# Attention with keys on partitions: scores computed transposed, the row maximum subtracted inside the fifth score pass

## The chip, the core and the metric

The kernel runs on one NeuronCore of a Trainium2 chip, as one program. The metric is the device time of one execution in microseconds. The median of three runs of the kernel before is given below, and beside it the time of the one execution that was profiled. In the profile PE is TensorE's matmul stream and PEld its weight loads, DVE is VectorE, ACT is ScalarE, POOL is GpSimd, SP is SyncE, which issues the DMAs.

## The reference, cut to what matters

The model is a two-layer backbone over 1024 latent tokens and 256 context tokens of width 1024. Layer 0 is a bidirectional gated linear recurrence (HGRN2), layer 1 is multi-head latent attention with 16 heads. Only the attention of layer 1 is touched. For each head it computes, with a score scale of (128 + 64) ** -0.5:

```python
s = (jnp.einsum('bqhd,bkhd->bhqk', q_nope, k_nope, preferred_element_type=jnp.float32)
     + jnp.einsum('bqhr,bkr->bhqk', q_pe, k_pe, preferred_element_type=jnp.float32))
p = jax.nn.softmax(s * MLA_SCALE, axis=-1)
return jnp.einsum('bhqk,bkhd->bqhd', p.astype(v.dtype), v)
```

Queries are the 1024 latent tokens (8 tiles of 128), keys are all 1280 tokens (10 tiles of 128). The output of each head is multiplied by a SiLU gate `z` and goes into the last projection `w_mo`.

## The kernel before

Products that must keep float32 accuracy are made of three passes: each operand is split into a high part in `float32r` and a low part (the rest), and `mm3` (line 261) adds high x high, low x high and high x low in PSUM. `split` (line 208) makes the parts: ScalarE copies the high part, VectorE subtracts it. The keys are shared by all heads, since the key projection is absorbed into the queries: `kh` and `kl` are the parts of the latent keys with their 128 channels on partitions, `kr` holds the rope keys, high part in partitions 0 to 63 and low part in 64 to 127. `vh` and `vl` are the latent values, with tokens on partitions.

The program runs through the stages one after the other: HGRN2, its output projection, `mla_in` (line 670: latent keys, values and query latents), `mla_rope` and `mla_z` (rope queries and gates, both put into DRAM), then `attend` (line 930), and the last projection.

`attend` writes the order of the attention stage by hand. Every step of four generators gets a due time in units of a query tile; the steps are sorted by it and run, and TensorE keeps that order (`AT_ORDER`, line 1284). The order of VectorE, ScalarE, GpSimd and SP is chosen by the framework, with two priorities (`AT_PRIO`, `EXP_PRIO`) as hints. The generators are:

- `attn_prep` (line 783), once a head: loads the head's weights `wk`, its gates `z` and, for every second head, the rope queries `qr`; forms the absorbed weight (line 800), transposes rope queries (line 818) and splits them into `rh` and `rl`, with a copy of the high part in the other partition half on GpSimd (`TWIN`, line 826); and forms the absorbed queries `qah` and `qal`.
- `attn_scores` (line 839), once a query tile: three blocks of keys (512, 512 and 256 columns), each with five matmuls (lines 855 to 859) whose stationary operand is the query tile, so that the scores lie with queries on partitions and keys along the row. VectorE reduces each block (line 861) and joins the three (line 867). The scale is negative, so the minimum is taken and handed to the exponential as a bias (line 871), and ScalarE's accumulator gives the row sums. VectorE then multiplies the 1280 probabilities by the reciprocal of the sum (line 882).
- `attn_values` (line 885), once a unit of two query tiles: five times four transposes of probabilities by TensorE (line 902) into `pt`, their split into `ph` and `pl` from PSUM, and six matmuls into `pv`. Then ScalarE copies the result and its high part (lines 920 and 921), GpSimd forms the low part `ol` (line 922), three matmuls apply the value projection, VectorE multiplies by `z` (line 927), and the result is stored in DRAM.
- `tail`: the first half of the last projection for two token tiles, woven into the end of the stage.

PSUM has eight banks of 512 float32 a partition: four for scores (`s`), three for `pt`, one for `pv`.

Of the kernel before, what the change touches and what calls it, by code (L numbers as in the profile page):

```python
# [18 lines left out]
P = 128  # L19
# [18 lines left out]
class Net:  # L38
# [631 lines left out]
    def mla_in(self, pool, pp, kp, a, hh, hl, st):  # L670
# [6 lines left out]
        for c in range(NT):  # L677
# [39 lines left out]
            )  # L717
            if lat:
# [64 lines left out]
    def attn_prep(self, pool, pp, a, st, qrD, zT, h, box):  # L783
# [23 lines left out]
        if h % 2 == 0:  # L807
# [6 lines left out]
            for b, n in self.qgs:  # L814
                sl = slice(b * P, (b + n) * P)
                ps = t(pp, [P, 512], F32, G_TAG)
                for j in range(n):
                    nc.tensor.transpose(ps[:, j * P : (j + 1) * P], qr[:, b + j], self.ident)
                for i, (rh, rl) in enumerate(box["pair"]):
                    own, twin = (slice(0, 64), slice(64, P))[:: 1 - 2 * i]  # L820
                    src = ps[own, : n * P]
                    nc.scalar.activation(rh[own, sl], src, AF.Copy, scale=SCALE)
# [16 lines left out]
    def attn_scores(self, pool, pp, st, box, i, prs):  # L839
        nc, t, NT = self.nc, self.t, self.NT  # L840
        mm = nc.tensor.matmul
        LK = NT * P
        blocks = [(o, min(512, LK - o)) for o in range(0, LK, 512)]
        nb = len(blocks)
        h, j = divmod(i, self.NL)
        qah, qal, rh, rl = box[h][:4]
        js = slice(j * P, (j + 1) * P)
        mx = t(pool, [P, 4], F32, "mx")
        sm = t(pool, [P, 4], F32, "sm")
        pr = t(pool, [P, LK], F32, "pr")  # L850
        sc = []
        for b, (o, w) in enumerate(blocks):
            s = t(pp, [P, 512], F32, "s")
            ks = slice(o, o + w)
            mm(s[:, :w], qah[:, js], st["kh"][:, ks], start=True, stop=False)  # L855
            mm(s[:, :w], qah[:, js], st["kl"][:, ks], start=False, stop=False)  # L856
            mm(s[:, :w], qal[:, js], st["kh"][:, ks], start=False, stop=False)  # L857
            mm(s[:, :w], rh[:, js], st["kr"][:, ks], start=False, stop=False)  # L858
            mm(s[:, :w], rl[:, js], st["kr"][:, ks], start=False, stop=True)  # L859
            with self.tc.high_priority(offset=AT_PRIO):  # L860
                nc.vector.tensor_reduce(mx[:, b : b + 1], s[:, :w], AX.X, ALU.min)  # L861
            sc.append(s)
            if b < nb - 1:
                yield
        nm = t(pool, [P, 1], F32, "nm")
        with self.tc.high_priority(offset=AT_PRIO):
            nc.vector.tensor_reduce(nm, mx[:, :nb], AX.X, ALU.min)  # L867
        for b, (o, w) in enumerate(blocks):
            yield
            with self.tc.high_priority(offset=EXP_PRIO):  # L870
                nc.scalar.activation(  # L871
                    pr[:, o : o + w], sc[b][:, :w], AF.Exp, bias=nm, scale=-1.0,
                    accum_out=sm[:, b : b + 1],
                )
        yield
        rs = t(pool, [P, 1], F32, "rs")
        nc.vector.tensor_reduce(rs, sm[:, :nb], AX.X, ALU.add)
        nc.vector.reciprocal(rs, rs)
        if i % NORM_ACT[1] < NORM_ACT[0]:
            nc.scalar.activation(pr, pr, AF.Copy, scale=rs)  # L880
        else:
            nc.vector.tensor_scalar(pr, pr, rs, None, ALU.mult)
        prs[i] = pr

    def attn_values(self, pool, pp, st, box, u, prs, yT):
        nc, t, NT = self.nc, self.t, self.NT
        tiles = [i for i in (2 * u, 2 * u + 1) if i < self.NH * self.NL]
        h, b = divmod(tiles[0], self.NL)
        n = len(tiles)
        N = n * P  # L890
        wvh, wvl, z = box[h][4:]
        np_ = -(-NT // 2)
        parts = {}
        acc = None
        for e in range(np_ + PV_LAG):
            if e < np_:
                m = min(2, NT - 2 * e)
                tp = t(pp, [P, 2, 2 * P], F32, "pt")
                for c in range(m):
# [491 lines left out]
```

## Time and profile before

| what | value |
|---|---|
| median of the runs | 3146.2 us (3143.35 to 3147.53, 3 runs) |
| time of the profiled execution | 3146.84 us |
| its span, first to last instruction | 3145.1 us |
| mean granted TensorE clock | 0.995 |
| busy share PE, DVE, ACT, POOL | 99%, 69%, 55%, 6% |
| first and last score matmul of the attention stage | 2130.8 and 2949.2 us |
| DMA, mean | 70 GB/s |

A row of a timeline gives start, duration, engine, line, operation, the tiles that it writes and reads, their shape, and in brackets the idle time ahead of it with its releaser. A row for one line gives the count, then the shortest, median and longest duration in nanoseconds, and the first and last start. Matmuls overlap in TensorE's pipeline, so the distance between two starts is the cost of one in a dense stream. A duration on VectorE or GpSimd runs from dispatch to completion and can hold waiting time. `f32` in a shape also stands for `float32r` operands of a matmul.

### The profile page before, as it was taken

The page shows a single profiled execution, that of the slowest core. Times are in us where ns is not written, and L with a number is a line of the kernel's source. Part 1 is how long each engine was busy: PE and PEld are TensorE (multiplying, and loading weights), DVE is VectorE, ACT ScalarE, POOL GpSimd, SP SyncE. Part 2 cuts the span into 40 slices and gives each one's busy share as a digit, 9 for nine tenths or more (in the row PEclk, how much of TensorE's full clock was granted, in tenths as well). Part 3 has the DMA queues.
Part 4 walks back from the last instruction along what each step waited for, and adds up shares of the span by engine and source line. Part 5 has one row for each costly group of instructions (what it writes and reads, how often), then busy time and mean ns, then how long its engine had stood idle before and what let it go on. Part 6 is the DMA issues. An engine that isn't in the chain of part 4 may idle for free.

```text
span 3145.1 us, 51475 instructions
## 1 busy us (share of the span) xinstructions
PE 3108.3 (99%) x19412; PEld 2782.5 (88%) x19412; DVE 2164.4 (69%) x4898; ACT 1729.6 (55%) x4263; POOL 188.3 (6%) x305
## 2 busy tenths in 40 slices
PE   8899999999999999999999999999999999999999
PEld 7889989899898998988988888788999999999887
DVE  7777688776886758757585563536777777777642
ACT  6556465564655646655475563224666666666532
POOL 0000000000000000000000011000010000000000
PEclk8999999999999999999999999999999999999999
DMA  5110212102111021010127661430101011101261
GB/s 212 43 56 23 74 36 63 56 23 75 36 56 57 24 73 36 30 40 25 41 69 243 222 197 45 141 117 24 41 30 38 24 34 34 34 28 38 69 219 57
DMA packets 100009, 218.88 MB, mean 70 GB/s; under 512 B 10289, under 2 KB 47409, under 8 KB 99761
## 3 DMA queue, kind: packets, MB, share of 16 engines
q1 hardware_dynamic: 99760, 215.59, 21.1%
q8 instruction: 153, 2.51, 0.3%
q14 instruction: 96, 0.78, 0.1%
HBM read 175.70 MB, written 39.85 MB: 69 GB/s over the span
## 4 chain that ended last, share of the span: by engine, by line
PE 92%; DVE 3%; issue 2%; DMA 2%; ACT 1%; POOL 0%; SPq 0%; DVEq 0%; POOLq 0%; ACTq 0%
PE g L265 12%; PE g L264 12%; PE g L263 12%; PE lv L335 6%; PE pt L902 4%; PE o L486 3%; PE pv L263 2%; PE s L855 2%; PE pv L264 2%; PE pv L265 2%; PE s L856 2%; PE s L858 2%; PE s L859 2%; PE s L857 2%; PE lv L263 2%; PE lv L265 2%
## 5 line engine op out<-in xcount | busy, mean ns | idle before, releaser
L263 PE MATMUL g<-hh,wh 128*128 128x512 f32 (+1 forms) x1512 | 548.4, 363 | 3.3 <-DVE hh L253 1.6
L265 PE MATMUL g<-hl,wh 128*128 128x512 f32 (+1 forms) x1512 | 542.4, 360 | 3.0 <-DVE hl L254 3.0
L264 PE MATMUL g<-hh,wl 128*128 128x512 f32 (+1 forms) x1512 | 543.3, 359 | 0.0
L263 PEld LDWEIGHTS g<-hh,wh 128*128 128x128 f32 x1512 | 286.5, 189 | 40.6 <-DVE hh L253 2.0
L265 PEld LDWEIGHTS g<-hl,wh 128*128 128x128 f32 x1512 | 285.7, 189 | 39.0 <-DVE hl L254 3.8
L215 DVE TENSOR_TENSOR wl<-raw,wh 128x1024 fp32r<-128x1024 f32 (+1 forms) x170 | 207.7, 1224 | 160.8 <-ACT wh L214 149.4
L264 PEld LDWEIGHTS g<-hh,wl 128*128 128x128 f32 x1512 | 286.4, 189 | 35.9
L861 DVE TENSOR_REDUCE mx<-s 128x1 f32<-128x512 f32 (+1 forms) x384 | 229.7, 599 | 94.5 <-PE s L859 93.0
L871 ACT ACTIVATE pr<-s,nm 128x512 f32<-128x512 f32 (+1 forms) x384 | 232.7, 615 | 99.1 <-DVE nm L867 92.8
L335 PE MATMUL lv<-QX,KX 128*128 128x128 f32 x1920 | 263.1, 275 | 5.8 <-ACT QX L407 4.3
L335 PEld LDWEIGHTS lv<-QX,KX 128*128 128x128 f32 x1920 | 246.6, 192 | 14.8 <-ACT QX L407 5.5
L214 ACT CAST wh<-raw 128x1024 fp32r<-128x1024 f32 (+1 forms) x170 | 178.0, 1049 | 121.8 <-PE lv L264 38.2
L214 ACT CAST ph<-pt 128x512 fp32r<-128x512 f32 x320 | 187.8, 587 | 96.2 <-PE pt L902 86.6
L215 DVE TENSOR_TENSOR pl<-pt,ph 128x512 fp32r<-128x512 f32 x320 | 219.4, 686 | 12.6 <-ACT ph L214 12.5
L263 PE MATMUL g<-wh,hh 128*128 128x256 f32 (+2 forms) x676 | 197.6, 293 | 0.0
L263 PE MATMUL pv<-ph,vh 128*128 128x256 f32 x640 | 196.7, 307 | 0.0
L265 PE MATMUL g<-wl,hh 128*128 128x256 f32 (+2 forms) x676 | 196.4, 291 | 0.0
L902 PE MATMUL pt<-ident,pr 128*128 128x128 f32 x1280 | 192.5, 273 | 0.1
L264 PE MATMUL g<-wh,hl 128*128 128x256 f32 (+1 forms) x654 | 187.9, 287 | 0.0
L407 ACT COPY KX<-K 128x256 f32<-128x256 f32 (+1 forms) x288 | 109.6, 381 | 131.3 <-PE lv L335 71.3
L265 PE MATMUL pv<-pl,vh 128*128 128x256 f32 x640 | 180.2, 282 | 0.0
L264 PE MATMUL pv<-ph,vl 128*128 128x256 f32 x640 | 180.0, 281 | 0.0
(557 smaller groups left out, 7918.3 us busy)
## 6 DMA issues: line engine op xcount, KB each, us to landing
raw<-in_w_o SPq DMA_DIRECT2D x64, 512.0 KB, 3.8
raw<-in_w_qfbz SPq DMA_DIRECT2D x61, 512.0 KB, 3.8
raw<-in_ada_wT SPq DMA_DIRECT2D x32, 512.0 KB, 3.6
raw<-in_w_mo SPq DMA_DIRECT2D x24, 512.0 KB, 3.9
raw<-in_w_v SPq DMA_DIRECT2D x16, 512.0 KB, 3.6
yT<-Z SPq DMA_DIRECT2D x32, 256.0 KB, 2.0
raw<-in_w_z SPq DMA_DIRECT2D x16, 512.0 KB, 4.1
pyr<-yT SPq DMA_DIRECT2D x64, 128.0 KB, 3.7
```

The costliest lines, as they stand in the source:

```text
L214: nc.scalar.copy(hi, src)
L215: (eng or nc.vector).tensor_tensor(lo, src, v32(hi), ALU.subtract)
L263: mm(ps, lh, rh, start=first, stop=False)
L264: mm(ps, ll, rh, start=False, stop=False)
L265: mm(ps, lh, rl, start=False, stop=last)
L335: nc.tensor.matmul(ps[:, sl], lhs[:, sl], rhs[:, sl], start=True, stop=True)
L407: cp(m12(N[:]), m12(Y))
L486: nc.tensor.matmul(o[:, sl], l, r, start=i == 0, stop=i == len(ops) - 1)
L855: mm(s[:, :w], qah[:, js], st["kh"][:, ks], start=True, stop=False)
L861: nc.vector.tensor_reduce(mx[:, b : b + 1], s[:, :w], AX.X, ALU.min)
L871: nc.scalar.activation(pr[:, o : o + w], sc[b][:, :w], AF.Exp, bias=nm, scale=-1.0, accum_out=sm[:, b : b + 1],)
L902: nc.tensor.transpose(tp[:, c, j * P : (j + 1) * P], prs[i][:, k * P : (k + 1) * P], self.ident)
```

## The change

The attention is written anew, in units of two query tiles of one head (64 units).

- `attn_scores` takes a block of two key tiles at a time, five blocks a unit. The stationary operand is now the key tile (`kh`, `kl`, `kh`, `kr`), the moving one the 256 queries, so that scores lie with keys on partitions. Four passes are accumulated. VectorE takes a running maximum over the five blocks, element by element, in `m2`, and joins its halves into `mf`. TensorE transposes `mf`, VectorE reduces it to one maximum a query (`mr`), TensorE spreads it over partitions with a matmul against an identity, and ScalarE copies it, negated, into row 64 of `rl`. A new key tensor `k5` has the rope keys' high part in rows 0 to 63 and ones in row 64, so the fifth pass (`k5` x `rl`) adds the rope queries' low part and subtracts the maximum. Then the exponential is taken without bias or accumulator, into `p`. The scale is positive now.
- The sums over keys are taken by GpSimd, which adds the five blocks of `p` and their halves into `l` (four buffers), and by a matmul of `l` with a column of ones in `attn_values`. The reciprocals go to DRAM as a row and come back spread over all partitions (`rb`), and GpSimd multiplies the finished output by them. The probabilities are not normalised before.
- `attn_split` splits `p` from SBUF into `ph` and `pl`. There are no transposes of probabilities.
- `ol` is formed by VectorE instead of GpSimd.
- `attend` runs a fixed loop: in iteration u the scores of unit u, the split of unit u-1, the value product of unit u-2 and the output of unit u-3. TensorE, VectorE, ScalarE and GpSimd all keep the program's order (`AT_HAND`).
- PSUM: four banks `s` and one `s5` for scores, one each for `pt`, `pv` and `mt` (the maximum).
- In `attn_prep` the two ScalarE copies of a rope block stand ahead of the VectorE and GpSimd steps. `mla_in` makes `k5` with one more ScalarE copy a tile.

The diff, cut to its core:

```diff
+            nc.scalar.copy(st["k5"][:64, sl], tp[:64, P : 2 * P])
...
+        for e in range(nb):
+            m = min(2, NT - 2 * e)
+            s = t(pp, [P, 512], F32, "s" if e < 4 else "s5")[:, : 2 * N].rearrange("p (a q) -> p a q", a=2)
+            for c in range(m):
+                ks = slice((2 * e + c) * P, (2 * e + c + 1) * P)
+                o = s[:, c]
+                for i, (l, r) in enumerate(((kh, qah), (kl, qah), (kh, qal), (kr, rh))):
+                    mm(o, l[:, ks], r[:, js], start=c + i == 0, stop=c == m - 1 and i == 3)
+            sc.append((m, s))
             with self.tc.high_priority(offset=AT_PRIO):
+                if e:
+                    nc.vector.tensor_tensor(m2[:, :m], m2[:, :m], s[:, :m], ALU.max)
+                else:
+                    nc.vector.tensor_copy(m2[:, :m], s[:, :m])
+            if e < nb - 1:
                 yield
+        mt = t(pp, [P, 2, 2 * P], F32, "mt")
...
+                nc.vector.tensor_tensor(mf, m2[:, 0], m2[:, 1], ALU.max)
+        yield
+        for j in range(n):
+            nc.tensor.transpose(mt[:, 0, j * P : (j + 1) * P], mf[:, j * P : (j + 1) * P], self.ident)
+        mr = t(pool, [P, n], F32R, "mr")
+        with self.tc.high_priority(offset=AT_PRIO):
+            nc.vector.tensor_reduce(mr, mt[:, 0, :N].rearrange("p (j k) -> p j k", k=P), AX.X, ALU.max)
+        yield
+        for j in range(n):
+            mm(
+                mt[:, 1, j * P : (j + 1) * P], mr[:, j : j + 1].broadcast_to([P, P]), self.identr,
+                start=True, stop=True,
+            )
+        with self.tc.high_priority(offset=AT_PRIO):
+            nc.scalar.activation(rl[64:65, js], mt[64:65, 1, :N], AF.Copy, scale=-1.0)
+        yield
+        ps = []
+        for e, (m, s) in enumerate(sc):
+            for c in range(m):
+                ks = slice((2 * e + c) * P, (2 * e + c + 1) * P)
+                mm(s[:, c], st["k5"][:, ks], rl[:, js], start=False, stop=c == m - 1, skip_group_check=True)
+            p = t(pool, [P, 2, N], F32, "p")
             with self.tc.high_priority(offset=EXP_PRIO):
+                nc.scalar.activation(p[:, :m], s[:, :m], AF.Exp)
+            ps.append((m, p))
+        cell["ps"], cell["parts"] = ps, []
+        add = nc.gpsimd.tensor_tensor
...
+            add(l2, whole[0], whole[1], ALU.add)
+            for p in whole[2:]:
+                add(l2, l2, p, ALU.add)
...
+            add(l, l2[:, 0], l2[:, 1], ALU.add)
...
+    def attn_split(self, pool, n, cell):
...
+        m, p = cell["ps"].pop(0)
+        ph = self.t(pool, [P, 2, n * P], F32R, "ph")
+        pl = self.t(pool, [P, 2, n * P], F32R, "pl")
+        self.split(ph[:, :m], pl[:, :m], p[:, :m])
...
+        for m, ph, pl in cell["parts"]:
+            for c in range(m):
+                self.mm3(acc[:, :N], st["vh"][:, k], st["vl"][:, k], ph[:, c], pl[:, c], k == 0, k == NT - 1)
+                k += 1
             yield
...
+        nc.scalar.copy(o32, acc[:, :N])
+        nc.scalar.copy(oh, o32)
+        yield
+        nc.vector.tensor_tensor(ol, o32, v32(oh), ALU.subtract)
         yield
         ps = t(pp, [P, 512], F32, G_TAG)
+        for j in range(n):
+            nc.tensor.matmul(
+                ps[:, 2 * P + j : 2 * P + j + 1], cell["l"][:, j * P : (j + 1) * P], self.ones, start=True, stop=True
+            )
+        self.mm3(ps[:, :N], wvh, wvl, oh, ol, True, True)
+        rc = t(pool, [P, n], F32, "rc")
+        nc.vector.reciprocal(rc, ps[:, 2 * P : 2 * P + n])
+        row = self.lD[u : u + 1, :N]
+        nc.sync.dma_start(row.rearrange("o (j p) -> p (o j)", p=P), rc)
+        rb = t(pool, [P, N], F32, "rb")
+        nc.sync.dma_start(rb, row.broadcast_to([P, N]))
+        y = t(pool, [P, N], F32, "ya")
+        nc.vector.tensor_tensor(y, ps[:, :N], z[:, b * P : b * P + N], ALU.mult)
+        yield
+        nc.gpsimd.tensor_tensor(y, y, rb, ALU.mult)
+        nc.sync.dma_start(yT[h][:, b * P : b * P + N], y)
...
+        for u in range(total):
+            cur = nxt = None
+            low, old = vals.get(u - 2), vals.pop(u - 3, None)
...
+            for e in range(nb):
+                if cur:
+                    next(cur)
+                if nxt and low and e in PREP_AT:
+                    next(nxt, None)
+                if old and e == min(LOW_AT, nb - 1):
+                    next(old)
+                if e in SPLIT_AT:
+                    split(u - 1)
...
+            split(u - 1)
+            for e in range(nb):
+                if low:
+                    next(low)
+                elif nxt and e in PREP_AT:
+                    next(nxt, None)
+                if not cur and e % 2:
+                    next(tail, None)
+                if e == min(2, nb - 1):
+                    if cur:
+                        next(cur)
+                    while cells.get(u - 1, {}).get("ps"):
+                        split(u - 1)
+                if e == min(3, nb - 1):
+                    if old:
+                        next(old)
+                    if cur:
+                        next(cur)
+            for _ in cur or ():
+                pass
+            if low:
+                next(low)
+            for _ in old or ():
+                pass
...
+    "qr": 1, "wk": 2, "qrh0": 2, "qrl0": 2, "qrh1": 2, "qrl1": 2, "p": 7, "ph": 9, "pl": 9,
+    "m2": 2, "mf": 2, "mr": 2, "l2": 2, "l": 4, "rc": 2, "rb": 2, "wvh": 3, "wvl": 3, "ya": 2, "oh": 2, "ol": 2,
...
+AT_PSUM = {"pt": 1, "pv": 1, "mt": 1, "s5": 1}
+PREP_AT = (1, 3)
+SPLIT_AT = (2, 3)
+LOW_AT = 2
+SCALE = float((128 + ROPE) ** -0.5)
+AT_HAND = {mybir.EngineType.PE, mybir.EngineType.DVE, mybir.EngineType.Activation, mybir.EngineType.Pool}
```

More of the change, by code (lines that the diff above doesn't have):

```diff
@@ L851, in attn_scores @@
         sc = []
[L852 to L859, printed above, removed]
-            with self.tc.high_priority(offset=AT_PRIO):
-                nc.vector.tensor_reduce(mx[:, b : b + 1], s[:, :w], AX.X, ALU.min)
-            sc.append(s)
-            if b < nb - 1:
+        m2 = t(pool, [P, 2, N], F32, "m2")
@@ L935, in attend @@
-        steps = []
+        units = [(h, b, min(2, NL - b)) for h in range(NH) for b in range(0, NL, 2)]
+        nb = -(-self.NT // 2)
+        per = -(-NL // 2)
+        prep = {}
         for h in range(1, NH):
-            t0 = NL * (h - 1) + 3 + AT_LAG
-            g = self.attn_prep(pool, pp, a, st, qrD, zT, h, box)
-            gap = min(0.9, (NL - 4 - AT_LAG) / 5)
-            steps += [(t0 + (e + (PREP_LATE if e > 1 and h % 2 == 0 else 0)) * gap, g) for e in range(6)]
-        nb = -(-self.NT * P // 512)
@@ L951, in attend, with split @@
-        steps += [(n + TAIL_AT + TAIL_GAP * k, tail) for k in range(NH)]
-        steps = sorted(enumerate(steps), key=lambda x: (x[1][0], x[0]))
-        for _, (_, g) in steps:
-            next(g, None)
+            prep[h] = self.attn_prep(pool, pp, a, st, qrD, zT, h, box)
+        cells, vals = {}, {}
+        total = len(units) + 2
+        def split(u):
+            if 0 <= u < len(units) and cells[u]["ps"]:
+                self.attn_split(pool, units[u][2], cells[u])
+        for u in range(total):
+            cur = nxt = None
+            low, old = vals.get(u - 2), vals.pop(u - 3, None)
+            if u < len(units):
+                h, b, n = units[u]
+                cells[u] = {}
+                cur = self.attn_scores(pool, pp, st, box, h, b, n, cells[u])
+                vals[u] = self.attn_values(pool, pp, st, box, h, b, n, u, cells[u], yT)
+                nxt = prep.get(u // per + 1)
+            for e in range(nb):
[7 more added lines that the diff above has]
+                    split(u - 1)
+            if nxt and u % per == per - 1:
+                for _ in nxt:
+                    pass
[22 more added lines that the diff above has]
+            for _ in old or ():
+                pass
+            cells.pop(u - 2, None)
@@ L957 @@
+        for x in vals.values():
+            for _ in x:
+                pass
+        for _ in tail:
+            pass
 VEC = {}
@@ L1259 @@
 K_LEAD = 8
-PREP_LATE = 0.5
 TWIN = lambda nc: nc.gpsimd.tensor_copy
```

133 lines of the change are left out of this document (44 added, 89 removed).

## The prediction, written before the result was known

> **What bounds the kernel now.** I read the page's engine shares first, then the table by stretches for the middle of the attention stage, then the score matmuls' own line, and last the timelines of single engines.
>
> ```profile
> PE 3108.3 (99%) x19412; PEld 2782.5 (88%) x19412; DVE 2164.4 (69%) x4898; ACT 1729.6 (55%) x4263; POOL 188.3 (6%) x305
> ```
>
> ```profile
> 2200.00:2900.00 700.00, 699.47 (x4767) 640.01 (x4766) 547.96 (x1168) 438.13 (x1127) 58.80 (x82) 1.00 0.11 33
> ```
>
> ```profile
> L855 PE MATMUL s<-kh,wl x384: 277/394/561, 2130.8 to 2948.7; 128*128 128x512 f32 x128, 128*128 128x256 f32 x64
> ```
>
> In the stretch (columns: length, then busy time of PE, PEld, DVE, ACT, POOL, the clock, DMA) TensorE is busy 699.47 of 700 us at clock 1.00, VectorE 547.96, GpSimd 58.80. So this stage lasts as long as TensorE's queue. Its 64 units (two query tiles of one head) take 2948.7 - 2130.8 = 817.9 us, 12.78 each. Matmuls overlap, so the distance of two starts, not the duration, is what one costs:
>
> ```profile
> 2506.01 0.28 PE L855 MATMUL s<-kh,wl 128*128 128x256 f32 x1
> ...
> 2506.60 0.39 PE L855 MATMUL s<-kh,wl 128*128 128x512 f32 x1
> ...
> 2507.76 0.28 PE L263 MATMUL pv<-ph,vh 128*128 128x256 f32 x1
> ...
> 2508.47 0.60 PE L902 MATMUL pt<-ident,pr 128*128 128x128 f32 x4
> 2508.82 0.48 PE L855 MATMUL s<-kh,wl 128*128 128x512 f32 x1
> 2509.14 0.39 PE L856 MATMUL s<-kl,wl 128*128 128x512 f32 x1
> ```
>
> Five matmuls of 256 columns take 0.59 us (0.118 each), five of 512 take 1.16 (0.232), six of the value product 0.71 (0.118). Four transposes take 0.35, and the matmul behind them starts its successor 0.32 later instead of 0.232: 0.09 for the change of kind, 0.44 in all. A unit is 2 x (10 x 0.232 + 5 x 0.118) = 5.82 for scores, 5 x 0.44 = 2.20 for transposes, 30 x 0.118 = 3.54 for values, three output matmuls 0.35: 11.91. A head's preparation (four pieces of 128 columns for the absorbed weights and four transposes for rope, 0.44 each, and 12 x 0.232) is 3.66, or 0.92 a unit. Sum 12.83, against 12.78 measured: the account closes.
>
> **The change on TensorE.** Scores come out with keys on partitions, so the 20 transposes of a unit go: -2.20. Four passes and the fifth are 50 matmuls of 256 columns: 5.90 instead of 5.82. New are two transposes of the maximum, two broadcast matmuls and two sums against a column of ones in plain float32, which the trace records as two pieces each:
>
> ```profile
> 32.49 0.50 PE L163 MATMUL lv<-csil,adap 128*128 128x2 f32 x4
> 32.85 0.49 PE L265 MATMUL g<-hl,wh 128*128 128x512 f32 x1
> ```
>
> ```profile
> 2992.82 1.95 PE L193 MATMUL acc<-ident,mod 128*128 128x128 f32 x16
> 2994.53 0.47 PE L264 MATMUL s<-wh,pyl 128*128 128x512 f32 x1
> ```
>
> Transposes 0.18 + 0.09; broadcasts 2 x 1.71/16 = 0.21; sums 0.36 + 0.09. With 3.54 + 0.35 unchanged a unit is 10.72, with preparation 11.64: 1.14 less than 12.78, or 73 us over 64 units, if TensorE stays dense. That is the second case below, not my forecast.
>
> **The loop that the maximum closes.** Before, the maximum of a tile was awaited by ScalarE alone. Now TensorE, in written order, waits for it: after four passes and three of five value steps it transposes `mf`, and behind that in its queue lie the other value steps, the output and the fifth pass. VectorE is in written order too, and ahead of `mf` stand a copy, four maxima, `ol` (moved here from GpSimd) and two `pl`. Prices of its operations, the hand-overs, and ScalarE's exponentials:
>
> ```profile
> 2503.32 0.15 DVE L877 TENSOR_REDUCE rs<-sm 128x1 f32<-128x3 f32 x1
> 2503.50 0.17 DVE L878 RECIPROCAL rs<-rs 128x1 f32<-128x1 f32 x1
> ...
> 2506.48 0.28 PE L859 MATMUL s<-kr,qrl 128*128 128x256 f32 x1
> 2506.80 0.42 DVE L861 TENSOR_REDUCE mx<-s 128x1 f32<-128x256 f32 x1
> ...
> 2510.58 0.68 DVE L215 TENSOR_TENSOR pl<-pt,ph 128x512 fp32r<-128x512 f32 x1
> 2511.18 0.68 DVE L861 TENSOR_REDUCE mx<-s 128x1 f32<-128x512 f32 x1
> ```
>
> ```profile
> 2135.65 0.69 ACT L871 ACTIVATE pr<-s,nm 128x512 f32<-128x512 f32 x1 [2.79 <-DVE nm L867]
> 2136.24 0.19 ACT L871 ACTIVATION_READ_ACCUMULATOR pr<-s,nm 128x1 f32 x1
> 2136.48 0.50 PE L855 MATMUL s<-kh,wl 128*128 128x512 f32 x1 [0.51 <-ACT pr L871]
> ```
>
> ```profile
> 2511.04 0.37 ACT L920 COPY o<-pv 128x256 f32<-128x256 f32 x1 [1.21 <-PE pv L265]
> ```
>
> A 512-wide VectorE operation lasts 0.69 (a median of 0.687 stands further below) and hides 0.08 behind its successor; 256-wide 0.42; a dependent one starts 0.03 after the end. VectorE starts 0.04 after a matmul's end, TensorE 0.14 after what it awaits. The exponentials lose their accumulator read and follow each other at 0.59. Busy time alone says little: five passes over the maximum and five `pl` at 0.69, four operations of 0.42, a reciprocal and preparation (0.86, below) are some 9.6 us of VectorE a unit, while before it was 547.96/700 x 12.78 = 10.0; the removed normalisation pays for the maxima. What counts is the order.
>
> I walk a unit without preparation, t = 0 at its first score matmul. Five key blocks of 8 x 0.118 = 0.944 are ready for VectorE at 1.15, 2.09, 3.03, 3.98 and 4.92; the third maximum ends at 3.72. Unhindered: `ol` 3.64 to 4.06, `pl` to 4.66, maximum to 5.26, `pl` to 5.86, maximum to 6.46, `mf` 6.49 to 6.91, TensorE at 7.05. TensorE's own work ahead is 4.72 + 18 x 0.118 = 6.84, so the cover just holds. From there 0.27 + 0.71 + 0.45 + 0.35 + 0.21 + 0.71 + 1.18 = 3.88 of TensorE work follow (the maximum's reduction and the ScalarE copy of 0.37 lie beside it), and 0.08 until the first exponential frees its bank: a period of 11.01.
>
> **What hinders it.** GpSimd now adds the exponentials of the unit before, in exactly these microseconds, and `pl`, `ol` and `mf` now read two SBUF tensors (`pl` had one in PSUM). What that does stands in a handful of rows:
>
> ```profile
> L922 POOL TENSOR_TENSOR ol<-o,oh x64: 730/737/1078, 2162.2 to 2984.5; 128x256 fp32r<-128x256 f32 x64
> L215 DVE TENSOR_TENSOR pl<-pt,ph x320: 670/687/694, 2147.2 to 2977.5; 128x512 fp32r<-128x512 f32 x160
> ...
> L215 DVE TENSOR_TENSOR wvl<-wv,wvh x16: 280/282/294, 2078.5 to 2877.8; 128x128 fp32r<-128x128 f32 x16
> ```
>
> ```profile
> 2214.96 0.88 DVE L882 TENSOR_SCALAR pr<-pr,rs 128x1280 f32<-128x1280 f32 x1
> 2215.41 1.02 POOL L922 TENSOR_TENSOR ol<-o,oh 128x256 fp32r<-128x256 f32 x1 [4.58 <-issue]
> ...
> 2983.46 1.23 DVE L215 TENSOR_TENSOR wl<-raw,wh 128x1024 fp32r<-128x1024 f32 x1 [1.96 <-ACT wh L214]
> 2984.53 0.76 POOL L922 TENSOR_TENSOR ol<-o,oh 128x256 fp32r<-128x256 f32 x1 [18.59 <-ACT oh L921]
> 2984.61 0.96 DVE L215 TENSOR_TENSOR pyl<-pyr,pyh 128x256 fp32r<-128x256 f32 x1
> ```
>
> The GpSimd operation of 0.737 became 1.02 beside a VectorE one that ended at 2215.84: it did 0.59 of work after that, 0.15 is its start. The VectorE operation of 0.42 became 0.96 beside GpSimd: it began in truth at 2985.57 - 0.42 = 2985.15, 0.14 before GpSimd's end, and at the hand-over (2984.69) GpSimd went first. With one operand in PSUM the 320 `pl` never passed 0.694. So the two engines exclude each other for operands in SBUF. The Trainium skill says so too (SBUF — State Buffer, section "SBUF: two separate sides": whichever of the two starts first holds the shared ports for its whole instruction); the trace has the hold ending 0.14 early. By the page's whole instruction each wait below would be about 0.28 longer, 0.56 a unit, and the sum 35 us more; I stay with the rows.
>
> A GpSimd addition of 512 has no row: between 0.74 (as 256) and 1.47 (twice); I take 0.15 + 2 x 0.59 = 1.33, since that row splits it; with the two of 256 it is 6.8 us of GpSimd a unit. The first starts when two exponentials are there, at 0.49, then one every 1.33; the third holds the ports from 3.30 to 4.34. `ol`, ready at 3.64, waits till then and ends at 4.76. If GpSimd's fourth goes first, as in the row, `pl` waits to 5.8, and with the sum of halves (0.74) behind it `mf` ends near 8.8 instead of 6.91: 1.9 more. If `pl` goes first, the addition falls beside a maximum and only the second `pl` waits: 8.3, 1.4 more. I take 1.6, between them: period 12.6. A gain is excluded here, the whole loss only if GpSimd's part is much shorter.
>
> Preparation puts VectorE work ahead of `mf`: a head has 0.28 + 0.42 + 2 x 0.69 and, halved over two heads, 4 x 0.69 for rope, some 0.75 a unit when packed; TensorE's 0.92 falls into the gap. Unit: 13.35. Two of the 64 have no values to work on and expose the whole chain, about 9.7 each (6.06 until `mf`, when VectorE does nothing else, and from there 3.6 for two transposes, reduction, broadcasts, copy and fifth pass with their hand-overs). 62 x 13.35 + 19.4 = 847, against 817.9: +29. The end has ScalarE and VectorE in written order as well, where weights of the last stage are split; between 0 and 6 (two passes over 1024 columns at the 1.23 quoted, and some waits), I take 3. Costed at nothing: `k5`'s extra copies, beside matmuls of a stage that TensorE leads; `pt` in one bank instead of three, since the next preparation step comes two key blocks (1.89) later and its reader needs under 0.7, and with the gap gone it would cost up to 0.5 in a few units of a head; the longer wait of `z`'s load in SP's queue, whose head is four units away. The reciprocals' row is the fourth case. Sum +32. The profiled execution took 3146.84 (span 3145.1), 0.64 over the median 3146.2; from the median: 3178.
>
> **The rivals.** *TensorE stays dense* (the other side): the ports decide nothing, because GpSimd's additions end before `ol` or VectorE goes first. For it: the unhindered walk meets TensorE's need within 0.2 us. Against: the 0.96 row. Units of 11.01 + 0.92 to 12.3 (with VectorE waiting for ScalarE in preparation) give 62 x 11.93 + 22.4 - 818 = -56, to -33: 3090 to 3113. The sign turns where 62 x (11.01 + 0.8 + w) + 22.4 = 818, at waits of w = 1.0 a unit. *Half held*: additions nearer 1.0, one wait of 0.8, preparation 0.84: 62 x 12.65 + 22.4 - 818 = -11, 3135. *The reciprocal's row through DRAM*: GpSimd's multiplication waits for two transfers; a store of this stage lands in
>
> ```profile
> yT<-ya SPq DMA_DIRECT2D x54, 128.0 KB, 1.8
> ```
>
> 1.8 each, 3.6 together, and some 10 us are free before its turn. 256 pieces of 4 bytes have no row; if they and SP's queue took 11 us, every unit would lose 1 more: 3240.
>
> **How the numbers follow.** Held ports 0.51 (3150 to 3212: 1.2 to 1.9 of waits, 1.2 where an addition is nearer 1.2, preparation 0.75 to 0.92, the end 0 to 6), dense 0.30, half held 0.14, the row 0.05. A change of 0.2% (6 us) is about what a measurement of this kernel can tell. Faster: 0.30 and two thirds of the half held, 0.39. Within 0.2%: 0.08, from the low edge of the held and the rest of the half held. Slower: 0.53. The range is 3088 to 3212; the held case alone is 3150 to 3212.
>
> **What would show it.** Right: TensorE idle about 1.5 us before the transpose of `mf`, released by VectorE, in nearly every unit; `pl` in the mean well over 0.69; GpSimd near 7 us a unit; the last score's start past 2950. Wrong: the stage in TensorE's section fully busy with `pl` at 0.69 (the dense case), or TensorE waiting for ScalarE's `rl` copy or GpSimd waiting for `rb`.

## The result, and the profile after

The changed kernel takes 3341.53 us (median of 4 runs, 3335.2 to 3343.22) against 3145.86 for the kernel before beside it: a ratio of 1.0619, 95% interval 1.0601 to 1.0637. It is slower, as forecast, but by 196 us instead of 32, beyond the upper end of the range, 3212.

The page's engine shares of the profiled execution (span 3341.4 us), the middle of the attention stage in the table by stretches, and the row of the score matmuls, each beside its counterpart in the prediction:

```profile
PE 3121.5 (93%) x19924; PEld 2827.4 (85%) x19924; DVE 2140.6 (64%) x4582; ACT 1680.6 (50%) x3889; POOL 575.3 (17%) x625
```

```profile
2200.00:2900.00 700.00, 596.58 (x4475) 572.33 (x4476) 449.74 (x770) 335.23 (x687) 327.77 (x299) 0.94 0.27 36
```

```profile
L859 PE MATMUL s<-wl,kh x640: 276/281/475, 2140.7 to 3082.6; 128*128 128x256 f32 x160
```

TensorE was busy 699.47 of these 700 us before and is busy 596.58 now. No engine took its place: VectorE, ScalarE and GpSimd are all below two thirds, so something passes the work around a loop in which each waits for another. The granted clock is 0.94 instead of 1.00. From the last row, and the ends of the spans, the loss can be laid out in three stretches. The last score matmul is counted by the first pass of the last block, as in the prediction (2948.7 before; its last pass starts at 2949.2):

| stretch | before | after | difference |
|---|---|---|---|
| start of the program to the first score matmul | 2130.8 | 2140.7 | +9.9 |
| first to last score matmul (64 units) | 817.9 (12.78 a unit) | 941.9 (14.72 a unit) | +124.0 |
| last score matmul to the end | 196.4 | 258.8 | +62.4 |

The sum, 196.3, is the difference of the spans. The forecast had +29 for the middle row (13.35 a unit where all steps run), +3 for the last, nothing for the first.

What the loop is shows in SP's queue. First the waits of that queue between 2300 and 3000 us (who waits, for whom; total, times, longest), then its timeline around one unit, then the transfers (count, KB each, median us from issue to landing):

```profile
SPq L958 <- DMA lD<-rc: 378.9, 46, 9.4
SPq L963 <- POOL ya L962: 234.0, 45, 6.9
```

```profile
2512.97 0.32 SPq L963 DMA_DIRECT2D yT<-ya  x1
2513.34 0.43 SPq L956 DMA_DIRECT2D lD<-rc  x1
2521.97 0.32 SPq L958 DMA_DIRECT2D rb<-lD  x1
2527.69 0.32 SPq L963 DMA_DIRECT2D yT<-ya  x1
2528.11 0.39 SPq L956 DMA_DIRECT2D lD<-rc  x1
```

```profile
rb<-lD SPq DMA_DIRECT2D x46, 128.0 KB, 4.9
yT<-ya SPq DMA_DIRECT2D x45, 128.0 KB, 1.8
...
lD<-rc SPq DMA_DIRECT2D x45, 1.0 KB, 8.6
```

SP waits for something during 613 of 700 us. Follow one round: the row of reciprocals is stored at 2513.34; the load of `rb` stands behind it and is issued only when the store has landed, 8.63 later; GpSimd starts its multiplication 4.95 after that; the output's store needs that result and is issued at 2527.69; and only behind it, at 2528.11, stands the next unit's row. This round is 14.77 us, and a unit of this kernel takes as much: from the first to the last transpose of a maximum, 2146.8 to 3086.6, the 63 distances are 14.9 us in the mean. The other engines show the same from their side, waits between 2300 and 3000 us and GpSimd's and VectorE's timelines:

```profile
POOL ya L962 <- issue: 157.7, 20, 10.0
DVE ya L960 <- DMA yT<-ya: 132.0, 30, 5.9
POOL ya L962 <- DMA rb<-lD: 88.7, 11, 9.1
ACT p L896 <- POOL l L904: 72.8, 34, 3.4
PEld mt L876 <- DVE mf L873: 58.3, 47, 2.8
PE mt L876 <- DVE mf L873: 48.9, 35, 2.6
```

```profile
2512.20 0.74 POOL L962 TENSOR_TENSOR ya<-ya,rb 128x256 f32<-128x256 f32 x1 [8.31 <-issue]
2512.90 1.26 POOL L904 TENSOR_TENSOR l<-p,p 128x512 f32<-128x512 f32 x1
...
2526.92 0.74 POOL L962 TENSOR_TENSOR ya<-ya,rb 128x256 f32<-128x256 f32 x1 [7.81 <-issue]
```

```profile
2509.10 0.16 DVE L954 RECIPROCAL rc<-pt 128x2 f32<-128x2 f32 x1
2514.84 0.42 DVE L960 TENSOR_TENSOR ya<-pt,za 128x256 f32<-128x256 f32 x1 [5.57 <-DMA yT<-ya]
```

The reciprocal was there at 2509.3, but its row left at 2513.34: SP stood at the output store of the unit before. GpSimd, in written order, holds the next additions behind the multiplication (2512.90), so the buffers of `p` come free late and ScalarE waits (72.8). VectorE, in written order, waits 5.57 before writing `ya`, which has two buffers, with the next unit's maxima behind it. TensorE waits for those (the rows of `mt` and `mf`).

### The profile page after: what moved, and what is told of

It reads as the page before. It is cut to its first block, busy times and chain, and to the rows that moved or that the text cites. A ratio compares the mean times of both kernels' runs of the same rounds, so it can differ in the third digit from the quotient of the medians.

```text
span 3341.4 us, 53078 instructions
## 1 busy us (share of the span) xinstructions
PE 3121.5 (93%) x19924; PEld 2827.4 (85%) x19924; DVE 2140.6 (64%) x4582; ACT 1680.6 (50%) x3889; POOL 575.3 (17%) x625
## 2 busy tenths in 40 slices
DMA packets 126641, 227.44 MB, mean 68 GB/s; under 512 B 28720, under 2 KB 74032, under 8 KB 126384
## 5 line engine op out<-in xcount | busy, mean ns | idle before, releaser
L81 POOL TENSOR_SCALAR rsq_m<-oss 128x4 f32<-128x4 f32 (+1 forms) x48 | 26.3, 548 | 1531.4 <-ACT ojunk L490 1531.4
L906 POOL TENSOR_TENSOR l<-l,p 128x512 f32<-128x512 f32 x192 | 252.5, 1315 | 15.1
L896 ACT ACTIVATE p<-s 128x512 f32<-128x512 f32 x320 | 172.9, 600 | 154.3 <-POOL l L904 86.0
L215 DVE TENSOR_TENSOR pl<-p,ph 128x512 fp32r<-128x512 f32 x320 | 249.3, 796 | 0.6
L859 PE MATMUL s<-wl,kh 128*128 128x256 f32 x640 | 190.8, 298 | 19.1 <-ACT p L896 19.1
L265 PE MATMUL g<-wl,hh 128*128 128x256 f32 (+2 forms) x676 | 196.4, 291 | 0.0
L214 ACT CAST ph<-p 128x512 fp32r<-128x512 f32 x320 | 177.7, 619 | 24.8 <-PE pv L264 24.3
```

Source lines behind the costliest of these rows:

```text
L81: nc.gpsimd.tensor_scalar(m, ss, 1.0 / n, EPS, ALU.mult, ALU.add)
L214: nc.scalar.copy(hi, src)
L215: (eng or nc.vector).tensor_tensor(lo, src, v32(hi), ALU.subtract)
L265: mm(ps, lh, rl, start=False, stop=last)
L859: mm(o, l[:, ks], r[:, js], start=c + i == 0, stop=c == m - 1 and i == 3)
L896: nc.scalar.activation(p[:, :m], s[:, :m], AF.Exp)
```

## The experiments

All kernels are compared with runs of the kernel before on the same chip (3145.86 to 3146.9 us in the median). "Stage" is the time from the first to the last score matmul in the profiled execution, as in the table; that execution can lie up to 9 us from the median given beside it.

**The row's trip left out.** GpSimd multiplies by a constant tile; nothing is stored and loaded.

```diff
-        row = self.lD[u : u + 1, :N]
-        nc.sync.dma_start(row.rearrange("o (j p) -> p (o j)", p=P), rc)
-        rb = t(pool, [P, N], F32, "rb")
-        nc.sync.dma_start(rb, row.broadcast_to([P, N]))
+        rb = self.rbc[:, :N]
...
```

> Leaves out the normalisation: GpSimd multiplies the output by a constant tile instead of the reciprocals, so the store of the reciprocals, their load and the wait for it are gone; all else is as in the changed kernel. Row-loop theory: one unit's period is the chain in SP's queue (store of 256 pieces 8.7 us, load 4.8, multiplication 0.74, issue of the output store 0.4, together 14.7), so without it the period falls to the next limit. Held-ports theory as the next limit: 12.6 to 13.9 a unit, total 3150 to 3215. TensorE dense as the next limit: 11.9 to 12.3 a unit, total 3090 to 3115. If the ports or the depth of the buffers of p set 14.7 by themselves, the total stays at 3320 to 3345.

Measured: 3259.5 us, ratio 1.0356 (1.0338 to 1.0373), stage 888.8. So 82 us of the 196 come back without the trip. The unit, 13.89, is at the upper end of the 12.6 to 13.9 expected; the time is 45 us above the 3150 to 3215, since that sum left out the start (+10.8) and the end (+34.3).

**The trip kept, but its use one unit later.** The generator's last step, multiplication and output store, runs in the next iteration, so that the round no longer closes within a unit.

```diff
-            for _ in old or ():
+            for _ in pend or ():
                 pass
+            pend = old
...
```

> The trip through DRAM stays as it is, with the full computation; only the last step of a unit (GpSimd's multiplication and the output store) is made one unit later, so that SP's queue holds store, load, then the output store of the unit before. Row-loop theory: a period of SP's queue is then 0.4 + 8.7 + 0.3 + 0.3 = 9.7 us, under the other limits, and the total is that of the run with the constant, within 20 us. If the transfers themselves or GpSimd's order were the cause, it stays at 3320 to 3345.

Measured: 3277.86 us, ratio 1.0412 (1.0383 to 1.0441), stage 891.7. It comes within the 20 us expected of the run above, though the row's store lands as late as before (8.3 us in the median): a slow store costs little once nothing in the unit waits for its round.

**More buffers alone.** `ya`, `rb` and `rc` get four buffers instead of two, `m2` and `l2` one.

```diff
-    "m2": 2, "mf": 2, "mr": 2, "l2": 2, "l": 4, "rc": 2, "rb": 2, "wvh": 3, "wvl": 3, "ya": 2,
+    "m2": 1, "mf": 2, "mr": 2, "l2": 1, "l": 4, "rc": 4, "rb": 4, "wvh": 3, "wvl": 3, "ya": 4,
```

> The changed kernel with four buffers instead of two for the output (ya), the spread reciprocals (rb) and the reciprocals (rc), paid for by one buffer instead of two for m2 and l2. VectorE's long wait is for a buffer of ya. Row-loop theory: a deeper queue does not raise the rate of a loop that is serial in SP's queue; unchanged, 3320 to 3350. Buffer theory: VectorE no longer waits, the period falls toward 13.4 and the total to 3180 to 3260.

Measured: 3299.7 us, ratio 1.0488 (1.0472 to 1.0503), stage 907. Both theories missed: 42 us came back, although more buffers do not open the round. The waits of SP's queue between 2300 and 3000 us:

```profile
SPq L958 <- DMA lD<-rc: 370.3, 47, 9.3
SPq L963 <- POOL ya L962: 244.1, 48, 5.7
```

SP still waits for 614 of 700 us, and rounds still follow each other without a pause: the row is stored at 2498.30, 2512.37 and 2526.39. But these rounds take 14.1 and 14.0 us instead of 14.77: the load follows its store after 8.0 instead of 8.63 (the median landing is 8.2 instead of 8.6). VectorE's wait for `yT`'s store is gone; whether that depth of buffers cost anything by itself, and why the store lands sooner, the runs do not show.

**The trip replaced, full computation.** TensorE spreads the reciprocals by a matmul against the identity, ScalarE copies them out of PSUM.

```diff
+        sp = t(pp, [P, 2, 2 * P], F32, "mt")
+        for j in range(n):
+            nc.tensor.matmul(
+                sp[:, 0, j * P : (j + 1) * P], rc[:, j : j + 1].broadcast_to([P, P]), self.ident, start=True, stop=True
+            )
+        rb = t(pool, [P, N], F32, "rb")
+        nc.scalar.copy(rb, sp[:, 0, :N])
         nc.gpsimd.tensor_tensor(y, y, rb, ALU.mult)
```

> Full computation without DRAM: the two reciprocals of a partition are spread over all partitions by two matmuls against the identity, ScalarE copies the result to SBUF, GpSimd multiplies as before. TensorE gets four pieces of 128 columns more a unit (0.4 to 0.5 us), ScalarE 0.4. Row-loop theory: as the run with the constant, up to 30 us above it (the whole 0.45 x 64 where TensorE is the bound, nearly nothing where VectorE is). Held ports next: 3150 to 3220. If the trip is not the cause: 3320 or more.

Measured: 3243.07 us, ratio 1.0303 (1.0286 to 1.0321), stage 868.9. About 98 us are gone. That is 16 us below the run with the constant, which has less to do (the last section has a part of the reason), and 23 us above the 3150 to 3220 expected of held ports, since start (+8.6) and tail (+27.8) are lost here too. This kernel's timeline, one unit, shows the mechanism that the prediction was built on:

```profile
2501.14 4.11 POOL L906 TENSOR_TENSOR l<-l,p 128x512 f32<-128x512 f32 x3
...
2503.36 0.74 DVE L945 TENSOR_TENSOR ol<-o,oh 128x256 fp32r<-128x256 f32 x1
2504.03 1.77 DVE L215 TENSOR_TENSOR pl<-p,ph 128x512 fp32r<-128x512 f32 x1
...
2507.63 0.42 DVE L873 TENSOR_TENSOR mf<-m 128x256 f32<-128x256 f32 x1
...
2508.20 0.41 PE L876 MATMUL mt<-ident,mf 128*128 128x128 f32 x2 [1.55 <-DVE mf L873]
```

GpSimd's three additions run to 2505.25. `pl` takes 1.77 instead of 0.69 and ends at 2505.80; counted back by its 0.69 it began at 2505.11, 0.14 before GpSimd's end. `ol` takes 0.74 instead of 0.42. TensorE then waits 1.55 for `mf`; its next wait there is again 1.55, at 2520.95, so the unit without preparation is 12.75 us.

**GpSimd's additions cut to 8 columns**, on top of the run before. The sums over keys are left out.

```diff
-            add(l2, whole[0], whole[1], ALU.add)
+            w = slice(0, 8)
+            add(l2[:, :, w], whole[0][:, :, w], whole[1][:, :, w], ALU.add)
...
-            add(l, l2[:, 0], l2[:, 1], ALU.add)
+        l = self.rbc
...
```

> The kernel with the reciprocals spread by TensorE (the run before, 3243.07 us, 13.58 a unit), but GpSimd adds only 8 of the 256 columns of each key tile and not the halves, and the sums are taken of a constant: the sums over keys are left out. Held ports: with GpSimd's operations short nothing holds VectorE, the 1.55 us gap of TensorE before the transposes of mf goes, pl comes back to 0.69 us in the mean (0.84 in the run before), and a unit takes TensorE's own 10.72 + 0.45 for the spread + 0.9 for preparation, 12.1 to 12.3: 3140 to 3170 us. Rival, VectorE's own queue is too long, whoever adds: the gap stays above 1 us and the time at 3230 to 3250.

Measured: 3162.06 us, ratio 1.0049 (1.0034 to 1.0064), stage 798.2. The subtractions on VectorE between 2300 and 2900 us (count, then shortest, median, longest in ns):

```profile
L215 DVE TENSOR_TENSOR pl<-p,ph x239: 681/684/694, 2301.3 to 2898.8; 128x512 fp32r<-128x512 f32 x120
```

No `pl` is longer than 0.694 us now; in the run before the longest took 1.775. TensorE's waits for `mf` between 2300 and 2900 us fall from 55.1 us (43 times) to 14.4 (19 times). VectorE's queue is unchanged, only GpSimd's work is shorter. Buffers of `p` that come free sooner are not the reason: in the run before, ScalarE had no wait for GpSimd's additions.

**The same done by order, full computation.** On top of the spread, `ol` and all five `pl` stand behind `mf` in VectorE's order: two `pl` behind the reduction to `mr`, three behind the multiplication by `z`.

```diff
-        self.split(ph[:, :m], pl[:, :m], p[:, :m])
+        self.nc.scalar.copy(ph[:, :m], p[:, :m])
+        cell["low"].append((pl[:, :m], p[:, :m], v32(ph[:, :m])))
...
+                    self.attn_low(cells.get(u - 1, {}), 2)
...
+                    self.attn_low(cells.get(u - 1, {}), 5)
...
-LOW_AT = 2
+LOW_AT = 4
```

> The same kernel with reciprocals spread by TensorE, full computation, with VectorE's ol and all five pl of a unit moved behind mf in its written order (two behind the reduction, three behind the multiplication by z). Held ports: ahead of mf only mf itself reads two SBUF tensors, so at most one addition (1.33) delays it; TensorE's gap falls from 1.55 to 0 to 0.6, a unit to 12.1 to 12.8: 3150 to 3195 us. Rival, VectorE's load is the bound and the moved pl only push the next unit's maxima back: a unit stays above 13.2, 3220 to 3260.

Measured: 3139.55 us, ratio 0.9978 (0.9967 to 0.9988), stage 777.7. Its subtractions in the same stretch:

```profile
L932 DVE TENSOR_TENSOR pl<-p,ph x245: 674/682/692, 2307.8 to 2899.2; 128x512 fp32r<-128x512 f32 x123
```

GpSimd adds as much as ever, and no `pl` is held; `mf` and `ol` are held only now and then (0.426 and 0.419 us in the median, 0.931 and 0.952 at most). A change of place alone is worth 104 us in the medians. It also shortens VectorE's queue ahead of `mf`, but the prediction's walk had that queue, unhindered, within 0.2 us a unit of TensorE's need, so that little of the 104 can be this. The stage fell by 91.2 us, to 12.15 a unit, at the short end of the 12.1 to 12.8 expected, and the time is 10 us below its range.

**No pair of SBUF operands ahead of the maximum at all.** The five `pl` stay behind the maximum, `ol` returns to its old place. `ol` reads the accumulator in PSUM, the copy `o32` goes, the maximum is taken 256 wide against PSUM, and the join of halves goes.

```diff
...
-                    nc.vector.tensor_tensor(m2[:, :m], m2[:, :m], s[:, :m], ALU.max)
...
+                for c in range(0 if e else 1, m):
+                    nc.vector.tensor_tensor(mf, mf, s[:, c], ALU.max)
...
-        nc.vector.tensor_tensor(ol, o32, v32(oh), ALU.subtract)
+        nc.vector.tensor_tensor(ol, acc[:, :N], v32(oh), ALU.subtract)
...
```

> The same, full computation, with ol in its old place but computed from the PSUM accumulator instead of its SBUF copy (that copy goes), and the maximum taken 256 wide, two steps a block, always against PSUM, so that the join of halves mf goes. Only the five pl, behind the maximum, read two SBUF tensors. Held ports: nothing ahead of the maximum can be held; no gap before the transposes, unit 12.0 to 12.3: 3130 to 3165 us, 15 to 40 below the run that only moves the pl. Rival, VectorE's load: 10 maxima of 0.42 are 0.3 us more a unit than five of 0.69 and mf, so it is slower than that run by up to 20 us.

Measured: 3138.07 us, ratio 0.9971 (0.9961 to 0.998), stage 775.1. In the range, but the 15 to 40 us below the run before did not come: TensorE's waits for `mf` were down to 4.6 us between 2300 and 3000 us there, so little was left to win.

**The row's trip kept, only the order changed.** The edit of `ol` and `pl` put on the changed kernel as it stands, full computation.

> The changed kernel with its row through DRAM, full computation, and only ol and the five pl moved behind mf in VectorE's order (the edit that took 104 us off where the row was gone). If the loop through SP's queue sets the period, nothing in VectorE's order can shorten it: 14.5 to 14.8 a unit, 3320 to 3345 us. Rival, the two costs simply add and the held ports give theirs back here too: 3225 to 3265.

Measured: 3279.41 us, ratio 1.0421 (1.0405 to 1.0436), stage 883.0, 13.80 a unit. Neither theory said this. The waits of SP's queue and its transfers, between 2300 and 3000 us:

```profile
SPq L964 <- DMA lD<-rc: 366.0, 49, 8.3
SPq L969 <- POOL ya L968: 251.8, 49, 6.5
```

```profile
lD<-rc SPq DMA_DIRECT2D x49, 1.0 KB, 7.8
```

The queue still waits for 618 of 700 us, so its round still sets the unit and the two costs do not simply add (that would have been about 3240). But the round itself became shorter, the store landing in 7.8 instead of 8.6 us, as with more buffers. Why it lands sooner stays open here too.

**What makes the store slow.** First the row was stored from two rows of a constant, two pieces of 512 bytes, the reciprocals left out:

> The changed kernel, but the row in DRAM is stored from two rows of a constant (two pieces of 512 bytes) instead of from the column of reciprocals (256 pieces of 4 bytes): the reciprocals are left out, both transfers and their order stay. If the small pieces are the cost, the store lands in 1.8 to 2.5 us instead of 8.6, the loop through SP's queue takes about 8 us instead of 14.7, less than a unit, and the time is near that of the kernel without the row's trip (3259.5): 3245 to 3300 us. Rival, two dependent transfers cost this much whatever their pieces: 3315 to 3345.

Measured: 3271.1 us, ratio 1.0393 (1.0375 to 1.041). The figure is in the range but decides less than meant: with nothing to wait for, all 64 stores were issued between 17 and 58 us of the program, so this run shows only that the load of `rb` alone costs little (12 us over the run with the constant). The next run keeps the store in its place. Its two pieces hold the reciprocals of two queries, written by one more VectorE operation; the others are left out.

```diff
-        nc.sync.dma_start(row.rearrange("o (j p) -> p (o j)", p=P), rc)
+        two = cell["l"][:n, :P]
+        nc.vector.tensor_scalar(two, self.ident[:n, :P], rc[:n, 0:1], None, ALU.mult)
+        nc.sync.dma_start(row.rearrange("o (j p) -> (o j) p", p=P), two)
```

> The changed kernel with one more VectorE operation, of 2 partitions x 128, that multiplies two rows of the identity by the reciprocals of two queries and puts them where the sums were; the row in DRAM is stored from these two partitions (two pieces of 512 bytes) in the same place of SP's queue, after the reciprocals as before. The reciprocals of the other queries are left out. If the 256 pieces of 4 bytes are the cost, the store lands in 1.8 to 2.5 us, the loop is 2.2 + 4.8 + 0.74 + 0.8 = 8.5 us, under a unit, and the time is that of the run without the store in the loop (3271): 3255 to 3295 us. Rival, a store with a load behind it on the same row takes 6 us or more whatever its pieces: a loop of 12.5 or more, 3300 to 3345.

Measured: 3240.26 us, ratio 1.0302 (1.0285 to 1.032), stage 868.9, below the expected range and the same as with the spread on TensorE. SP's timeline, and its wait for that store between 2300 and 3000 us:

```profile
2516.45 0.32 SPq L965 DMA_DIRECT2D yT<-ya  x1
2519.46 0.24 SPq L958 DMA_DIRECT2D lD<-l  x1
2520.62 0.32 SPq L960 DMA_DIRECT2D rb<-lD  x1
```

```profile
SPq L960 <- DMA lD<-l: 35.8, 51, 0.9
```

The load follows its store after 1.16 us instead of 8.63, and SP waits 0.7 for it in the mean instead of 8.2. The whole execution moves 11440 packets under 512 bytes here, against 28720 in the changed kernel. The pieces are the cost, not the transfers.

**The best version, full computation.** On the PSUM version: the reciprocals spread by transposes, which the trace shows as one piece each; the first head's preparation alternates between `pt` and `s5`; and the tail's weights are loaded and split one step ahead, with its matmuls ahead of the value steps.

```diff
-            nc.tensor.matmul(
-                sp[:, 0, j * P : (j + 1) * P], rc[:, j : j + 1].broadcast_to([P, P]), self.ident, start=True, stop=True
-            )
+            nc.tensor.transpose(sp[:, 0, j * P : (j + 1) * P], rc[:, j : j + 1].broadcast_to([P, P]), self.ident)
...
+        tags = [G_TAG] if h else [G_TAG, "s5"]
...
+                if u == len(units) - 1 and e == 1:
+                    next(tail, None)
```

> Full computation. The run with the maximum and ol from PSUM (3138.07 us), and three more edits: the reciprocals are spread by two transposes (one piece of 0.09 each) instead of two plain matmuls (0.45 together), the preparation of the first head alternates between pt and s5, and the tail's loads are split one step ahead, the first in the last unit with scores, with its matmuls ahead of the value steps. If TensorE is the limit of every unit now, the transposes give 64 x 0.27 = 17 us; the first head's waits (2.9 and 1.4) give 4, the tail's waits (2.0, 0.3, 1.8, 1.6) 4 to 7: 3108 to 3116 us, with 3104 to 3120 for the uncertainty. Rival, the stage is now held by VectorE or by the exponentials: only start and tail come, 3126 to 3134.

Measured: 3106.8 us, ratio 0.9873 (0.9858 to 0.9888), stage 758.0, 11.84 a unit. The row by stretches:

```profile
2200.00:2880.00 680.00, 670.18 (x5556) 661.26 (x5557) 511.40 (x1161) 392.12 (x832) 390.53 (x367) 1.00 0.10 32
```

TensorE is busy 98.6% of it at clock 1.00. Against the version without these edits the stage fell by 17.1 (17 expected of the transposes) and the tail by 10.3. The start is 5.9 earlier, of which only 3.5 can be assigned (below). The time is 1 us under the 3108 to 3116 and inside the 3104 to 3120.

## Why the prediction was right and wrong, step by step

**What bounds the kernel before, and TensorE's account: right.** The account gave 11.64 a unit with preparation, once nothing waits. The PSUM version spreads the reciprocals for 0.45 more, which makes 12.09; its stage is 775.1 / 64 = 12.11. The best version spreads them for 0.18 and makes 11.82; measured 11.84. That both agree to 0.02 is in part luck: in the PSUM version TensorE is idle for 21 of the 775.1 us, 0.33 a unit, while the first two units have no values to multiply and the first head is prepared before the stage.

**The reciprocals' row: the step that failed.** It was costed at nothing, as a latency of 2 x 1.8 us with "some 10 us are free before its turn", and the rival that had it slower got 0.05 and 3240 us. Two things were wrong. The store in 256 pieces had "no row", and the nearest row, 1.8 us for 128 KB, was taken although the pieces were named as unlike it; it took 8.6, and the load of `rb` behind it took 4.9. And the trip was treated as a latency beside the unit, while store, load, multiplication, output store and the next row stand in one queue, each waiting for the one before, so that it is a loop with a period: 8.63 + 4.95 + 0.77 + 0.42 = 14.77 us. No free time inside the unit hides a loop that is longer than the unit. Writing down SP's queue for two units in a row would have shown the loop, even with the price unknown; with the other terms as measured afterwards, any landing beyond 5.9 us makes it longer than 12. The rival had the right sign, but it too took the trip for a wait inside the unit.

The Trainium skill (DMA: Bandwidth & Descriptors, section "Rules for kernel authors") says that a non-contiguous last dimension lowers to one descriptor per element. The runs agree: 8.6 us against about 1.2 for the same kilobyte in two pieces, and 28720 packets under 512 bytes against 11440.

The row is not all that was missed. With it gone, the kernel with the spread still takes 3243.07, above 3212: its span is 55 us longer than the forecast's, 22 in the stage (868.9 against 847, the spread included), 25 at the end and 9 at the start.

**Held ports: right, as the second cause.** With the row out of the way the changed kernel does what the walk said. The prediction had `pl` and `ol` waiting for GpSimd, `pl` beginning 0.14 before GpSimd's end, 1.4 to 1.9 of waits and 12.6 for a unit without preparation; the run has 0.14, 1.55 and 12.75, of which 0.45 is the spread, partly in the gap. In the run with the constant, which has no spread, the shortest units are 12.7. The estimate of 1.33 for an addition stands against 1.315 in the page of after:

```profile
L906 POOL TENSOR_TENSOR l<-l,p 128x512 f32<-128x512 f32 x192 | 252.5, 1315 | 15.1
...
L215 DVE TENSOR_TENSOR pl<-p,ph 128x512 fp32r<-128x512 f32 x320 | 249.3, 796 | 0.6
```

Two runs confirm it from both sides: less GpSimd work with VectorE's order untouched (-81 us), and the same work elsewhere in VectorE's order (-104). The dense case, "the other side", was therefore not wrong in kind: it is near what the same change gives without the two waits. That its 3090 to 3113 holds the best version's 3106.8 is partly luck, since that one has the start and the tail mended too.

**Preparation: 0.75 a unit, somewhat low.** In the run with the spread, (868.9 - 19.4) / 62 - 12.75 = 0.95.

**The end: 0 to 6 taken, 62 measured.** In the tail of the changed kernel TensorE's waits come to 43 us, and these are two of the three longest:

```profile
3095.45 0.58 PE L263 MATMUL pv<-ph,vh 128*128 128x256 f32 x1 [5.02 <-ACT o L942]
...
3124.88 0.79 PE L263 MATMUL s<-wh,pyh 128*128 128x512 f32 x1 [11.45 <-ACT pyh L214]
```

The loads of the last projection (weights and `yT`) lie in SP's queue behind the rows of the last units, and ScalarE and VectorE, in written order, stand with them. With the row gone the loss is 27.8; in the best version, with the loads ahead, 15.2, of which TensorE's waits are 7.6. The rest is not split.

**`pt` in one bank: costed at nothing beside the next preparation step.** That held inside the loop, not for the first head, whose steps follow each other without scores between them. After, at the first preparation:

```profile
2112.00 0.47 PE L263 MATMUL pt<-qh,wqh 128*128 128x512 f32 x1 [2.86 <-DVE qrl L826]
```

Rows for 2100 to 2130 us, of the changed kernel and of the best version, where a second bank is used there:

```profile
2100.00:2130.00 30.00, 25.74 (x105) 20.37 (x104) 8.56 (x11) 7.00 (x11) 2.43 (x4) 0.89 0.26 82
```

```profile
2100.00:2130.00 30.00, 29.21 (x131) 23.58 (x130) 9.15 (x12) 7.85 (x13) 2.43 (x4) 1.00 0.27 93
```

TensorE, busy all 30 us before, lost 4.3 of the 9.9 here, and the bank gave 3.5 back. The rest of the start stays open: the first score matmul came anywhere from 2134.0 to 2143.6 us in kernels whose code up to there is the same (and at 2145.8 where all the rows were stored at the program's start).

**The clock was not in the sum.** See the last section. At 0.94 over the middle of the stage it is a part of the 942 us; how large a part stays open.

**What would show it.** The signs named were partly the right ones: the prediction listed "GpSimd waiting for `rb`" among the things that would make it wrong, and that is what the waits of after show. The signs of the held case were there as well: TensorE idle before the transposes, released by `mf`, 35 times for 1.4 us in the mean, and `pl` at 0.796. They could not tell which of the two set the unit; SP's queue could.

## What to carry to other kernels

When a change adds a transfer whose result is awaited, write out the queue that issues it for two rounds: the sum of everything that waits for the one before is a period, and it competes with the period of the busiest engine, not with the free time of one round. Price a transfer by the number of its pieces as well as by its bytes, and spread a column by a transpose or a matmul rather than by a store in pieces. And where two engines cannot work at once on SBUF operands, the cheapest cure is to move the held operation behind the one that others wait for, or to read one operand from PSUM.

## What the runs showed of the hardware

**A stall can halve TensorE's clock for a few microseconds after it.** After, TensorE's timeline behind one wait:

```profile
2514.84 0.39 PE L859 MATMUL s<-wl,kh 128*128 128x256 f32 x1 [1.77 <-ACT p L896]
2515.06 0.28 PE L859 MATMUL s<-wl,kl 128*128 128x256 f32 x1
...
2515.83 0.41 PE L859 MATMUL s<-qrh,kr 128*128 128x256 f32 x1
2516.04 0.41 PE L859 MATMUL s<-wl,kh 128*128 128x256 f32 x1
...
2519.18 0.28 PE L859 MATMUL s<-qrh,kr 128*128 128x256 f32 x1
```

From 2515.83 to 2519.03 matmuls stand 0.213 apart instead of 0.118, and the granted clock of that stretch is 0.50; then full speed returns. Between 2300 and 2700 us of this kernel, none of the 18 waits of 0.5 to 1.6 us was followed by such a stretch, and at least 7 of the 20 longer ones (1.6 to 2.65) were. That is no threshold: in the run with the spread three waits of 1.55 were followed by one. Nor does every wait of such a length do it: in the same 400 us the run with the constant rows has 10 such stretches and the run with two pieces 4 (mean clock 0.93 and 0.97), with nearly the same waits (1.68 and 1.71 in the mean of those over 1 us).

That would explain a part of why the former is slower with less to do: by that spacing such a stretch costs some 1.4 us, so six more of them in 400 us make an estimated 19 of the 29 us between their stages (897.7 and 868.9). The runs in which the round no longer sets the unit lie roughly in that order: clock 0.98 with the spread (3243.07 us), 0.97 with two pieces (3240.26), 0.96 with the constant (3259.5), 0.94 with the use one unit later (3277.86) and 0.93 with the constant rows (3271.1). Why the stretches are more frequent in one than in another is not shown.

The Trainium skill (TensorE: Matmul & The Clock Gate, "What's actually happening") has half speed follow an idle window of about 3.4 us; here waits half as long were enough. The free-running window of the same section would fit that not every one counts, but no run here shows the window.

**The number of pieces, not of bytes, made a store slow:** 1 KB in 256 pieces landed in 8.6 us, 128 KB in 128 rows in 1.8, 1 KB in two pieces in at most 1.2.
